# PEER block on one core: u of 32 more tokens from gathered rows, a dense u over 352 columns, 64 blocks ahead that alternate in the output, and a packed slot sum

## The chip, the cores and the metric

The kernel runs on one core of a Trainium2 chip. Its time is the device time of one execution in microseconds. Three executions of the kernel before took 1765.59, 1766.91 and 1767.95 us, median 1766.91. One further execution was profiled. Engines are called by their names in the profile: PE multiplies matrices, DVE (vector), ACT (scalar) and POOL (GpSimd) work on elements, SP issues most DMAs; POOL issues the gathers.

## The reference

One layer over 512 tokens of 1024 features in float32. First come two mixers (attention in bands of chunks, and an mLSTM); this part of the kernel, the front, is the same before and after. Then come the product-key experts:

```python
def peer_ffn(h, w_pq, sub_keys, u_exp, v_exp):          # 512 tokens, in blocks of 128
    q = (xb @ w_pq).reshape(128, 8, 2, 128)             # 8 heads, 2 halves of a key
    s = jnp.einsum("thpd,hpnd->thpn", q, sub_keys)      # 128 sub-keys for each half
    s_top, i_top = lax.top_k(s, 16)
    cand = s_top[:, :, 0, :, None] + s_top[:, :, 1, None, :]
    best, ci = lax.top_k(cand, 16)                      # 16 experts for each head
    e = i1 * 128 + i2                                   # of 128 x 128 = 16384
    gate = softmax(best)
    u, v = u_exp[e], v_exp[e]                           # 16384 rows of 1024 each
    act = gelu(einsum("thkd,td->thk", u, xb))
    return einsum("thk,thkd->td", gate * act, v)
```

Each token so uses 128 rows of u and 128 rows of v, out of 16384 rows in each table.

## The kernel before

Tokens 0 to 127 take their rows by gathering: for each of the 128 picks, one indirect DMA brings one row of 1024 floats for each token (512 KB), and DVE multiplies it with the token's features and sums (u; a "dot", tile `junk`), or adds it with the gate as factor (v, `sum_v`). This is `gathered`.

The other 384 tokens go densely through all 16384 experts, in 128 blocks of 128 experts. For one block e, `hidden` loads 128 rows of u (512 KB, tile `wst`), splits them into a high and a low half (`split`: ACT copies, then one subtraction on DVE or POOL, as the list `lanes["now"]` says), and forms 8 x 3 products of 128x384 on PE (`mm3`: high·high, low·high and high·low make up the precision of float32; tile `ps_act`), then gelu on ACT. `output` does the same with v's block (tile `vst`), after the hidden values have been multiplied by the gate weights (`gq`, result `ew`) and split in turn (`ehi`, `elo`): 18 products of 128x512 on PE into six accumulators (`acc`).

The gate weights of the dense tokens are a matrix of 16384 experts by 384 tokens, which `build` makes from one-hots: for each token one 128x128 matrix `oa` (the gate at the first index) and for four tokens one `o4` (the second index), multiplied on PE into `ps_g`, copied by ACT and written to DRAM as `gd`, to be read back as `gq`.

The order of the work is the order of the program: generators that are advanced in turn. `scores` (queries, top 16, `select` of the slots) and then `build` of token blocks 1, 2 and 3 run beside `ahead`, which already forms hidden values of 40 expert blocks (E1), 8 of them kept in SBUF and 32 written to DRAM (`ad`, read back as `aq`). In `output` then come 88 blocks that have both u and v to do (hot), and after them the 40 that have only v to do (cold). The gathers of tokens 0 to 127 are issued beside the output, 2.5 for each block (RATE_V).

The tiles have a fixed number of buffers (six for a gathered row, UR; four for a v block, VST; five halves of a split block, WB); an instruction that wants a buffer waits until its last reader is done.

## Time and profile before

| | before |
|---|---|
| runs | 1765.59, 1766.91, 1767.95 us (median 1766.91) |
| profiled execution | 1767.14 us, its span 1765.3 us |
| PE busy | 1705.3 us (97%), granted clock 0.988 |
| DVE busy | 1380.5 us (78%) |
| POOL, ACT busy | 832.6 us (47%), 806.3 us (46%) |
| moved by DMA | 413.35 MB, mean 234 GB/s |

The profiled execution's time is 1.84 us more than the span from the first to the last instruction, and 0.23 us more than the median of the three runs. An engine's busy time is the time in which at least one of its instructions ran; successive instructions of one engine overlap a little, so that a stream's pace is read from the distance of the starts rather than from the durations.

### The profile page before, as it was taken

The page shows a single profiled execution, that of the slowest core. Times are in us where ns is not written, and L with a number is a line of the kernel's source. Part 1 is how long each engine was busy: PE and PEld are TensorE (multiplying, and loading weights), DVE is VectorE, ACT ScalarE, POOL GpSimd, SP SyncE. Part 2 cuts the span into 40 slices and gives each one's busy share as a digit, 9 for nine tenths or more (in the row PEclk, how much of TensorE's full clock was granted, in tenths as well). Part 3 has the DMA queues.
Part 4 walks back from the last instruction along what each step waited for, and adds up shares of the span by engine and source line. Part 5 has one row for each costly group of instructions (what it writes and reads, how often), then busy time and mean ns, then how long its engine had stood idle before and what let it go on. Part 6 is the DMA issues. An engine that isn't in the chain of part 4 may idle for free.

```text
span 1765.3 us, 25467 instructions
## 1 busy us (share of the span) xinstructions
PE 1705.3 (97%) x8671; PEld 1486.5 (84%) x8671; DVE 1380.5 (78%) x2868; ACT 806.3 (46%) x1624; POOL 832.6 (47%) x692
## 2 busy tenths in 40 slices
PE   5999999999999897999999999999999999999997
PEld 4766678888798787999899999999999999998886
DVE  7557655675589998899477988899989898898445
ACT  4544545443543334998533443433434443434443
POOL 0000000000157676999455666677776677673221
PEclk9999999999999998999999999999999999999999
DMA  8423224563332333565998989989999989987653
GB/s 292 152 73 127 88 99 140 186 227 100 111 104 89 104 101 135 204 255 233 343 367 322 358 308 344 352 324 342 348 326 351 353 303 351 350 293 282 228 194 107
DMA packets 129940, 413.35 MB, mean 234 GB/s; under 512 B 12049, under 2 KB 38801, under 8 KB 128274
## 3 DMA queue, kind: packets, MB, share of 16 engines
q1 hardware_dynamic: 91218, 252.33, 41.3%
q0 software_dynamic: 38592, 159.40, 24.1%
q8 instruction: 68, 1.11, 0.2%
q14 instruction: 62, 0.51, 0.1%
HBM read 376.03 MB, written 35.66 MB: 233 GB/s over the span
## 4 chain that ended last, share of the span: by engine, by line
PE 80%; DVE 13%; DMA 4%; issue 1%; POOL 1%; ACT 1%; SPq 0%; DVEq 0%; ACTq 0%
PE acc L165 10%; PE acc L164 10%; PE acc L163 10%; PE ps_act L165 8%; PE ps_act L163 8%; PE ps_act L164 8%; PE ps_g L766 4%; DVE wlo L153 2%; DMA wst<-in_w_ada 1%; PE ps_ya L361 1%; PE ps_s L341 1%; PE ps_qk L163 1%; DVE i L648 1%; PE ps_qk L165 1%; DVE sc L649 1%
## 5 line engine op out<-in xcount | busy, mean ns | idle before, releaser
L150 ACT CAST whi<-wst 128x512 fp32r<-128x512 f32 x408 | 252.1, 621 | 482.6 <-PE ps_act L164 279.6
L165 PE MATMUL ps_act<-h2T_hi,wlo 128*128 128x384 f32 x1024 | 348.3, 340 | 5.0 <-DVE wlo L153 4.0
L163 PE MATMUL ps_act<-h2T_hi,whi 128*128 128x384 f32 x1024 | 347.0, 339 | 0.0
L164 PE MATMUL ps_act<-h2T_lo,whi 128*128 128x384 f32 x1024 | 346.8, 339 | 0.0
L164 PE MATMUL acc<-wlo,ehi 128*128 128x512 f32 x768 | 299.1, 391 | 0.0
L163 PE MATMUL acc<-whi,ehi 128*128 128x512 f32 x768 | 293.3, 390 | 3.3 <-ACT whi L150 3.3
L165 PE MATMUL acc<-whi,elo 128*128 128x512 f32 x768 | 286.9, 391 | 0.0
L153 DVE TENSOR_TENSOR wlo<-wst,whi 128x512 fp32r<-128x512 f32 x275 | 207.0, 756 | 98.2 <-ACT whi L150 91.1
L153 POOL TENSOR_TENSOR wlo<-wst,whi 128x512 fp32r<-128x512 f32 x133 | 184.4, 1393 | 180.9 <-ACT whi L150 174.9
L150 ACT CAST whi<-vst 128x512 fp32r<-128x512 f32 x256 | 158.0, 620 | 181.2 <-PE acc L165 137.9
L724 POOL DMA_INDIRECT vr<-in_v_r,ei x128 | 168.6, 1317 | 84.5 <-DVE sum_v L730 65.9
L710 POOL DMA_INDIRECT ur<-in_u_r,ei x128 | 153.5, 1199 | 115.3 <-DVE junk L713 93.6
L153 POOL TENSOR_TENSOR wlo<-vst,whi 128x512 fp32r<-128x512 f32 x85 | 131.0, 1541 | 151.7 <-ACT whi L150 136.1
L165 PEld LDWEIGHTS ps_act<-h2T_hi,wlo 128*128 128x128 f32 x1024 | 193.8, 189 | 7.3 <-DVE wlo L153 5.2
L163 PEld LDWEIGHTS ps_act<-h2T_hi,whi 128*128 128x128 f32 x1024 | 194.0, 189 | 3.7
L164 PEld LDWEIGHTS ps_act<-h2T_lo,whi 128*128 128x128 f32 x1024 | 193.9, 189 | 3.7
L730 DVE SCALAR_TENSOR_TENSOR sum_v<-vr,act,sum_v 128x1024 f32<-128x1024 f32 x127 | 181.2, 1427 | 1.2 <-DMA vr<-in_v_r,ei 0.4
L713 DVE SCALAR_TENSOR_TENSOR junk<-ur,h 128x1024 bf16<-128x1024 f32 x128 | 170.9, 1335 | 0.9
L163 PEld LDWEIGHTS acc<-whi,ehi 128*128 128x128 f32 x768 | 144.6, 188 | 31.5 <-ACT whi L150 3.6
L165 PEld LDWEIGHTS acc<-whi,elo 128*128 128x128 f32 x768 | 144.0, 188 | 30.4 <-DVE elo L841 0.2
L164 PEld LDWEIGHTS acc<-wlo,ehi 128*128 128x128 f32 x768 | 144.1, 188 | 28.5
L471 POOL TENSOR_SCALAR_AFFINE_SELECT mbd<-mbc 128x512 f32<-128x512 f32 x4 | 4.7, 1163 | 319.5 <-ACT mbc L469 319.5
(300 smaller groups left out, 3103.8 us busy)
## 6 DMA issues: line engine op xcount, KB each, us to landing
wst<-in_u_t SPq DMA_DIRECT2D x128, 512.0 KB
vst<-in_v_e SPq DMA_DIRECT2D x128, 512.0 KB
wst<-in_w_pieces SPq DMA_DIRECT2D x76, 512.0 KB
wst<-in_w_ada SPq DMA_DIRECT2D x48, 512.0 KB
gd<-gst POOLq DMA_DIRECT2D x12, 2048.0 KB
gq<-gd SPq DMA_DIRECT2D x16, 1536.0 KB
ad<-gelu SPq DMA_DIRECT2D x8, 768.0 KB
aq<-ad SPq DMA_DIRECT2D x8, 768.0 KB
```

The costliest lines, as they stand in the source:

```text
L150: nc.scalar.copy(hi, t[:, cs])
L153: e.tensor_tensor(out=lo, in0=t[:, cs], in1=hi.bitcast(F32), op=ALU.subtract)
L163: nc.tensor.matmul(o, a[0], b[0], start=first, stop=False)
L164: nc.tensor.matmul(o, a[0], b[1], start=False, stop=False)
L165: return nc.tensor.matmul(o, a[1], b[0], start=False, stop=last)
L341: nc.tensor.matmul(pss[:, :n], qaT[po : po + 64, cs], kaT[po : po + 64, hp, :n], start=True, stop=True)
L361: nc.tensor.matmul(psy[po : po + 64, cs], va[:, kt, h * 64 : (h + 1) * 64], pt[:, kt * P : (kt + 1) * P], start=kt == 0, stop=kt == qt,)
L710: nc.gpsimd.indirect_dma_start(out=t, out_offset=None, in_=u_r, in_offset=bass.IndirectOffsetOnAxis(ap=ei[:, j : j + 1], axis=0))
L713: nc.vector.scalar_tensor_tensor(junk(), t, 1.0, state["h2"][i], op0=ALU.mult, op1=ALU.mult, accum_out=act[:, j : j + 1])
L724: nc.gpsimd.indirect_dma_start(out=t, out_offset=None, in_=v_r, in_offset=bass.IndirectOffsetOnAxis(ap=ei[:, j : j + 1], axis=0))
L730: nc.vector.scalar_tensor_tensor(sum_v, t, act[:, j : j + 1], sum_v, op0=ALU.mult, op1=ALU.add)
L766: nc.tensor.matmul(ps[:, tt::4], oa, ob, start=True, stop=True)
```

## The change

1. Tokens 128 to 159 (TG = 32) now take u, not v, from gathered rows. The new `group` lays their 128 picks out as four groups of 32 tokens over the 128 partitions, so that 32 indirect DMAs of 128 rows do for 32 tokens. It needs small DMAs for the indices (`eg`, four for each head), for the results (`at`) and for three copies of the tokens' features; the result is multiplied into the gate weights of these tokens before they go into `build`.
2. The dense u so covers 352 columns (NU) in place of 384. The dense v keeps 384 (ND).
3. 64 blocks go ahead in place of 40, none kept in SBUF. In the output, groups of 8 hot and 8 cold blocks alternate.
4. The gathers of tokens 0 to 127 start in the build of token block 1 (RATE_0), go on beside the rest of the blocks ahead (RATE_A), and then take 2.6 for each hot and 1.25 for each cold block. The rows of `group` are gathered in the builds of token blocks 2 and 3 (RATE_G). `slowly` lets each gather be issued after the last subtraction (or slot operation) that DVE had been given by then.
5. `split` makes one subtraction of 1024 columns after the scores, and two of 512 in them. Its lanes are POOL, POOL, DVE in the scores and DVE alone from then on, in the output too (before: DVE, POOL, POOL until the output, DVE, DVE, POOL in it). The output takes experts in pairs: one multiplication by the gate weights of 704 columns, one split of 768.
6. One-hots: ACT takes a second one of each 16 tokens (`tt == 2`), and none for tokens 128 to 159.
7. `select`: one sum over products carries both parts of the slot (factor 64), and five operations of 64 elements take them apart; one 128x1024 product on POOL and one 128x1024 sum on DVE are gone, and three casts and copies pass from DVE to POOL.
8. Buffers: v blocks 4 to 3, gathered rows 6 to 5, split blocks five halves to three wholes, o4 6 to 4, one-hots 6 to 8 (POOL) and 16 to 12.

```diff
-VST, UR = 4, 6
+VST, UR = 3, 5
-E1 = 40
+TG = 32
+NU = S - P - TG
+ND = S - P
+E1 = 64
-RATE_S, RATE_B, RATE_V = 1.0, 0.15, 2.5
+RATE_S, TOP, RATE_G, RATE_B, RATE_0, RATE_A, HOT, COLD = 1.1, 2, 0.65, 0.4, 0.8, 1.0, 2.6, 1.25
-LANES_F = lambda nc: [nc.vector, nc.gpsimd, nc.gpsimd]
-LANES_V = lambda nc: [nc.vector, nc.vector, nc.gpsimd]
+LANES_S = lambda nc: [nc.gpsimd, nc.gpsimd, nc.vector]
+LANES_B = lambda nc: [nc.vector]
...
+    def group(cp):
+        slots = state["slots"][:TG, 1]
...
+        for h in range(8):
+            et = cp.tile([TG, TOPK], I32, tag="et", name="et")
+            nc.vector.scalar_tensor_tensor(et, slots[:, 0, h], float(P), slots[:, 1, h], op0=ALU.mult, op1=ALU.add)
+            hs = slice(h * NJ, (h + 1) * NJ)
+            for g in range(NR):
+                nc.sync.dma_start(eg[g * TG : (g + 1) * TG, hs], et[:, g * NJ : (g + 1) * NJ])
+            yield
+            for j in range(NJ):
+                dot_u(cp, eg, h * NJ + j, state["h2"][1], ag)
+                yield
...
+            ins = e.tensor_tensor(out=lo[:, cs], in0=t[:, cs], in1=hi[:, cs].bitcast(F32), op=ALU.subtract)
+            if e is nc.vector:
+                state["mark"] = ins.ins
...
+    def slowly(g):
+        while True:
+            with tc.issue_after(state["mark"]):
+                ended = next(g, 0) == 0
...
+            for i in (2, 3, 1):
+                if i == 1:
+                    drive((rows, 1))
+                    gate = state["slots"][:TG, 1, 2]
+                    nc.vector.tensor_mul(gate, gate, state["at"])
+                own = (slowly(gather), RATE_0) if i == 1 else (slowly(rows), RATE_G)
+                drive((paced(build(dp, i, state["slots"][:, i]), (side, RATE_B), own), 1))
+            drive((paced(side, (slowly(gather), RATE_A)), 1))
...
-        order = list(range(E1, P)) + list(range(E1))
+        hot, cold = ([list(range(e, e + GG, 2)) for e in r] for r in (range(E1, P, GG), range(0, E1, GG)))
+        while hot or cold:
+            for g in (hot, cold):
+                order += g.pop(0) if g else []
...
+                yield HOT if e >= E1 else COLD
...
-                    if tt == 0 and t4 % ACT_D < ACT_N:
+                    if (tt == 0 or (tt == 2 and t4 % 4 == 0)) and i * P + t >= P + TG:
                         nc.scalar.activation(oa, iota, AF.Abs, bias=neg[:, 0, t : t + 1])
...
-        nc.vector.tensor_copy(idx, i16)
+        nc.gpsimd.tensor_copy(idx, i16)
...
-        nc.vector.tensor_reduce(slots[:, :, 0, h], q, axis=AX.X, op=ALU.add)
-        nc.gpsimd.tensor_mul(m, m, bq(C_DOFF))
-        nc.vector.tensor_reduce(of, m, axis=AX.X, op=ALU.add)
-        nc.vector.tensor_sub(of, pf, of)
+        both = cp.tile([P, 4, TOPK], F32, tag="both", name="both")
+        nc.vector.tensor_reduce(both, q, axis=AX.X, op=ALU.add)
+        nc.vector.tensor_scalar(of, both, 1.0 / PACK, WHOLE, op0=ALU.mult, op1=ALU.add)
+        nc.vector.tensor_scalar_add(slots[:, :, 0, h], of, -WHOLE)
+        nc.vector.scalar_tensor_tensor(of, slots[:, :, 0, h], float(PACK), both, op0=ALU.mult, op1=ALU.subtract)
+        nc.vector.tensor_add(of, of, pf)
...
-        ps = bank(tag, "ps_act")[:, :ND]
-        proj_t(ps, u, [t[:, :, GT:] for t in h2T])
+        ps = bank(tag, "ps_act")[:, :NU]
+        proj_t(ps, u, [t[:, :, S - NU :] for t in h2T])
```

DVE's program inside the build before (one-hots `oa` and `o`, a half split `wlo` now and then):

```order
L750 TENSOR_TENSOR o_7731<-iota,sT 128x512
L153 TENSOR_TENSOR wlo<-wst,whi 128x512
L764 TENSOR_SCALAR oa<-iota,sT 128x128 x2
L750 TENSOR_TENSOR o_7748<-iota,sT 128x512
L764 TENSOR_SCALAR oa<-iota,sT 128x128 x2
L750 TENSOR_TENSOR o_7767<-iota,sT 128x512
```

DVE's program at a place of the build after (the one-hots at L799 and L784, a whole split at L150, and the dots of the 32 tokens' gathered rows, `junk,ag`):

```order
L784 TENSOR_TENSOR o_6480<-iota,sT 128x512
L799 TENSOR_SCALAR oa<-iota,sT 128x128
L712 SCALAR_TENSOR_TENSOR junk,ag<-ur,h_1_3828 128x1024
L799 TENSOR_SCALAR oa<-iota,sT 128x128
L784 TENSOR_TENSOR o_6501<-iota,sT 128x512
L799 TENSOR_SCALAR oa<-iota,sT 128x128
L150 TENSOR_TENSOR wlo<-wst,whi 128x1024
L712 SCALAR_TENSOR_TENSOR junk,ag<-ur,h_1_3828 128x1024
L784 TENSOR_TENSOR o_6518<-iota,sT 128x512
L799 TENSOR_SCALAR oa<-iota,sT 128x128 x2
L784 TENSOR_TENSOR o_6573<-iota,sT 128x512
```

Between the one-hots there now stand dots and whole splits.

POOL's program in the output before (the v rows' gathers `vr`, and POOL's share of the subtractions):

```order
L153 TENSOR_TENSOR wlo<-vst,whi 128x512
L724 DMA vr<-in_v_r,ei_8700 128x1024 x5
L153 TENSOR_TENSOR wlo<-vst,whi 128x512
L153 TENSOR_TENSOR wlo<-wst,whi 128x512
L724 DMA vr<-in_v_r,ei_8700 128x1024
L153 TENSOR_TENSOR wlo<-wst,whi 128x512
L724 DMA vr<-in_v_r,ei_8700 128x1024
L153 TENSOR_TENSOR wlo<-vst,whi 128x512
L724 DMA vr<-in_v_r,ei_8700 128x1024 x7
```

POOL's program after, from the last one-hot on (the gate weights' writes `gd`, the gathers of u and then of v for tokens 0 to 127):

```order
L799 TENSOR_SCALAR oa<-iota,sT 128x128
L807 DMA gd<-gst 128x4096
L704 DMA ur<-in_u_r,ei_8277 128x1024 x5
L807 DMA gd<-gst 128x4096
L704 DMA ur<-in_u_r,ei_8277 128x1024 x100
L704 DMA ur<-in_v_r,ei_8277 128x1024 x128
```

The subtractions are gone from POOL's queue, and gathers follow one another.

## Rows read from the trace of the kernel before

**Rows 1.** The busy time of each engine in seven stretches of the span: the front (mixers), the scores, the building of the gate weights, the rest of the blocks ahead, the hot blocks of the output, its cold blocks, the tail. Columns: stretch, its length in us, then busy us and number of instructions of PE, PE's weight loads, DVE, ACT and POOL, PE's granted clock as a share, the DMA engines' busy share, GB/s.

```profile
0.00:467.90 467.90, 441.00 (x1993) 339.29 (x1993) 293.33 (x701) 214.98 (x453) 9.99 (x17) 0.98 0.44 148
467.90:704.90 237.00, 217.46 (x1127) 195.33 (x1127) 216.56 (x921) 95.20 (x180) 150.02 (x152) 0.96 0.31 102
704.90:846.10 141.20, 140.83 (x1083) 140.34 (x1082) 132.64 (x285) 128.86 (x319) 134.97 (x123) 1.00 0.61 236
846.10:875.00 28.90, 25.63 (x150) 25.31 (x149) 6.98 (x14) 10.95 (x22) 11.53 (x11) 1.00 0.93 340
875.00:1583.50 708.50, 708.50 (x3570) 644.37 (x3571) 622.46 (x777) 281.81 (x511) 481.53 (x362) 1.00 0.93 337
1583.50:1755.40 171.90, 171.86 (x758) 141.84 (x757) 102.06 (x161) 72.43 (x137) 44.60 (x29) 1.00 0.60 211
1755.40:1765.30 9.90, 0.00 (x0) 0.00 (x0) 6.42 (x15) 2.11 (x8) 0.00 (x0) 0.70 0.42 159
```

**Rows 2.** The chain of work that ended last, its shares of the span by engine (part 4 of the page).

```profile
PE 80%; DVE 13%; DMA 4%; issue 1%; POOL 1%; ACT 1%; SPq 0%; DVEq 0%; ACTq 0%
```

**Rows 3.** Waits in the whole span: who waited on which line, for whom; us in total, times, longest us.

```profile
POOL ur L710 <- DVE junk L713: 93.6, 68, 4.8
...
PE ps_slT L739 <- DVE slots L688: 7.5, 1, 7.5
```

**Rows 4.** Three rows of PE's timeline in the hot blocks (start us, duration us). Between the first and the second of them stand 13 more rows of ps_act, between the second and the third six more of acc, none with idle time before it.

```profile
999.78 0.33 PE L164 MATMUL ps_act<-h2T_lo,whi 128*128 128x384 f32 x1
...
1002.20 0.39 PE L163 MATMUL acc<-whi,ehi 128*128 128x512 f32 x1
...
1003.82 0.40 PE L164 MATMUL acc<-wlo,ehi 128*128 128x512 f32 x1
```

**Rows 5.** PE's groups in the stretch 875.0 to 1583.5 (hot blocks); two more groups of 674 and two of 516, one for each of the other two products, stand beside them. Columns: tiles and shapes, count, busy us, mean ns of one, idle us before them.

```profile
L163 PE MATMUL ps_act<-h2T_hi,whi 128*128 128x384 f32 x674 | 226.4, 336 | 0.0
...
L163 PE MATMUL acc<-whi,ehi 128*128 128x512 f32 x516 | 200.7, 391 | 3.3 <-ACT whi L150 3.3
```

**Rows 6.** The same in the stretch 1583.5 to 1755.4 (cold blocks); two more groups of 252 stand beside it.

```profile
L163 PE MATMUL acc<-whi,ehi 128*128 128x512 f32 x252 | 92.7, 389 | 0.0
```

**Rows 7.** DVE's groups in the stretch 467.9 to 704.9 (scores), shapes kept apart.

```profile
L153 DVE TENSOR_TENSOR wlo<-wst,whi 128x512 fp32r<-128x512 f32 x26 | 32.6, 1254 | 9.0 <-ACT whi L150 9.0
...
L690 DVE TENSOR_REDUCE of<-m 128x64 f32<-128x1024 f32 x8 | 9.6, 1200 | 0.0
L656 DVE CAST idx<-i 128x128 f32<-128x128 uint32 x8 | 7.0, 879 | 0.2
...
L670 DVE COPY dl<-idx 128x4 f32<-128x4 f32 x8 | 4.3, 535 | 0.1
...
L691 DVE TENSOR_TENSOR of<-pf,of 128x64 f32<-128x64 f32 x8 | 3.4, 428 | 0.0
...
L668 DVE CAST pf<-pos 128x64 f32<-128x64 uint32 x8 | 2.5, 314 | 0.2
```

**Rows 8.** One of POOL's groups in the same stretch.

```profile
L689 POOL TENSOR_TENSOR m<-m,cst 128x1024 f32<-128x1024 f32 x8 | 20.4, 2551 | 0.2
```

**Rows 9.** DVE's one-hots in the stretch 704.9 to 846.1 (build).

```profile
L764 DVE TENSOR_SCALAR oa<-iota,sT 128x128 f32<-128x128 f32 x185 | 74.3, 445 | 0.5 <-PE ps_g L766 0.5
L750 DVE TENSOR_TENSOR o<-iota,sT 128x512 f32<-128x512 f32 x90 | 64.6, 727 | 7.9 <-ACT sT L741 7.9
```

**Rows 10.** DVE's timeline inside the build (start us, duration us; x2 is two instructions drawn together).

```profile
721.14 0.59 DVE L764 TENSOR_SCALAR oa<-iota,sT 128x128 f32<-128x128 f32 x2
721.66 0.68 DVE L750 TENSOR_TENSOR o<-iota,sT 128x512 f32<-128x512 f32 x1
722.26 0.59 DVE L764 TENSOR_SCALAR oa<-iota,sT 128x128 f32<-128x128 f32 x2
```

**Rows 11.** One piece of the chain of waits in the build, in order of time (start us, length us).

```profile
758.27 1.78 PE ps_g L766 x16
```

**Rows 12.** DVE's timeline in the hot blocks.

```profile
998.87 2.35 DVE L153 TENSOR_TENSOR wlo<-vst,whi 128x512 fp32r<-128x512 f32 x1 [0.36 <-ACT whi L150]
1001.14 1.21 DVE L713 SCALAR_TENSOR_TENSOR junk<-ur,h 128x1024 bf16<-128x1024 f32 x1
...
1002.28 0.68 DVE L153 TENSOR_TENSOR wlo<-wst,whi 128x512 fp32r<-128x512 f32 x1
1002.89 1.21 DVE L713 SCALAR_TENSOR_TENSOR junk<-ur,h 128x1024 bf16<-128x1024 f32 x1
```

**Rows 13.** POOL's timeline in the same place.

```profile
999.35 1.30 POOL L153 TENSOR_TENSOR wlo<-vst,whi 128x512 fp32r<-128x512 f32 x1
```

**Rows 14.** DVE's two groups that read gathered rows, in the stretch 875.0 to 1583.5.

```profile
L730 DVE SCALAR_TENSOR_TENSOR sum_v<-vr,act,sum_v 128x1024 f32<-128x1024 f32 x121 | 171.5, 1417 | 1.2 <-DMA vr<-in_v_r,ei 0.4
L713 DVE SCALAR_TENSOR_TENSOR junk<-ur,h 128x1024 bf16<-128x1024 f32 x128 | 170.9, 1335 | 0.9
```

**Rows 15.** PE's timeline at the end of the scores, around its longest wait there.

```profile
686.10 0.48 PE L739 MATMUL ps_slT<-ident,slots 128*128 128x128 f32 x1 [7.51 <-DVE slots L688]
...
687.01 0.52 PE L163 MATMUL ps_act<-h2T_hi,whi 128*128 128x384 f32 x1
687.34 0.52 PE L164 MATMUL ps_act<-h2T_lo,whi 128*128 128x384 f32 x1
```

**Rows 16.** What the DMA engines moved, in 40 equal slices of the span, 44.1 us each (part 2 of the page).

```profile
GB/s 292 152 73 127 88 99 140 186 227 100 111 104 89 104 101 135 204 255 233 343 367 322 358 308 344 352 324 342 348 326 351 353 303 351 350 293 282 228 194 107
```

More of the change, by code (lines that the diff above doesn't have):

```diff
@@ L595, in branches @@
         h2T = features("h2T")
[L596 removed]
+        h2 = [hpool.tile([P, D], F32, tag=f"row{i}", name=f"h2_{i}") for i in range(2)]
         state["h2T"], state["h2"] = h2T, h2
@@ new lines, in output @@
+            whb, wlb = (x.rearrange("p i (b t) -> p b i t", t=TB) for x in (whi, wlo))
+            nc.scalar.copy(whb, w)
+            nc.vector.tensor_sub(wlb, w, whb.bitcast(F32))
+            for i in range(2):
+                v = split(load(v_e[e + i], "vst", VST, vp), vp, VB)
+                last = e == order[-1] and i == 1
+                late.append((e == order[0] and i == 0, last, whi[:, i, :], wlo[:, i, :], v))
+                if len(late) > 1 and not last:
+                    x = late.pop(0)
+                    for n in range(2):
+                        for j in range(nt):
+                            rows_of_v(j, n, *x)
+                yield HOT if e >= E1 else COLD
@@ L935, in tile_block @@
             nc.sync.dma_start(gtd, gt2[:1, :])
-            main, side = front(dp, dp, h2T), ahead(up, h2T, held)
-            lanes["now"] = LANES_F(nc)
-            n, due = 0, 0.0
-            for _ in main:
-                n += 1
-                due += RATE_S if n <= 16 else RATE_B
-                while due >= 1.0:
-                    due -= 1.0
-                    next(side, None)
-            drive((side, 1))
-            lanes["now"] = LANES_V(nc)
+            side, rows, gather = ahead(up, h2T), group(cp), gathered(cp, 0)
+            lanes["now"] = LANES_S(nc)
+            drive((paced(scores(dp, h2T), (side, RATE_S)), 1))
+            for _ in range(TOP):
+                next(side, None)
+            lanes["now"], state["cuts"] = LANES_B(nc), 1
+            for i in (2, 3, 1):
[6 more added lines that the diff above has]
+            drive((paced(side, (slowly(gather), RATE_A)), 1))
         if stop == "u":
             return
-        with pool("vpool") as vp, pool("rpool") as rp:
-            gather = gather_side(rp)
-            with tc.issue_after(state["marks"][MARK]):
-                next(gather)
-                next(gather)
-            paced(output(rp, vp, h2T, held), gather, RATE_V)
+        with pool("vpool") as vp:
+            drive((paced(output(cp, vp, h2T), (slowly(gather), None)), 1))
             drive((gather, 1))
```

209 lines of the change are left out of this document (102 added, 107 removed).

## The prediction

> **What bounds the kernel now.** I read the table of stretches first [rows 1]. From 875.0 to 1755.4 us PE is busy all the time (708.50 of 708.5 and 171.86 of 171.9 us), so the output is PE's own work. The build is nearly the same (140.83 of 141.2). In the scores PE idles 19.5 of 237.0 us; there DVE has 216.56 us of work and most of the chain. Over the whole span the chain is 80% PE and 13% DVE [rows 2]. The question is therefore what PE is given less of, and whether the engines that now serve it keep up.
>
> Next the pace of PE, from the distance of starts. Fourteen products of 384 columns take 1002.20 − 999.78 = 2.42 us, 173 ns each; seven of 512 take 1.62 us, 231 ns [rows 4]. Whole stretches are the better measure. The cold blocks give 171.9/(3 × 252) = 0.2274 us for 512 columns [rows 1, 6]. The hot blocks then give (708.5 − 1548 × 0.2274)/2022 = 0.1763 us for 384, waits included [rows 1, 5]. The slope is 0.0511/128 = 0.40 ns per column; the 32 columns are worth 12.8 ns, and one product of 352 should take 0.1635 us.
>
> **What leaves PE.** 128 blocks × 24 products × 12.8 ns = 39.3 us. v stays at 384 tokens, and the one-hot products stay. This is the only work that PE loses; all else moves work between stretches or between engines. The bounds are nothing saved and 0.45 ns per column, from the two timeline paces (231 − 173 over 128): 44 us.
>
> By the Trainium skill ("TensorE: Matmul & The Clock Gate", section Back-to-back issue gap) a sustained stream of weight loads and products is spaced by both, at about 81 ns for 128 columns and 131 ns for 512. Its slope, 0.13 ns per column, would make the saving only an estimated 13 us. The trace's 227 ns for 512 disagrees, so I take the rows.
>
> **Scores, 237.0 to about 239 us.** DVE sets the pace. Removed are the second sum L690 (9.6 us), the casts and copies (7.0, 4.3, 2.5) and L691 (3.4): 26.8 us [rows 7]. Added are 40 operations of 64 elements. L691, of this size, took 0.43 us with POOL busy beside it [rows 7]; `oa`, with twice the elements, stands 0.26 us from the next [rows 10]. I take 0.26, 10 us; the other end is 17. Program order puts 22 half and 10 whole subtractions there, in place of 26 halves: 22 × 1.254 + 10 × 1.2 − 32.6 = +7 us. Eight dots at 1.25 us add 10, four index operations about 1.5. The sum is 237.0 − 26.8 + 10 + 7 + 10 + 1.5 = 238.7. POOL loses L689 (20.4 us, [rows 8]) and gains the casts, which DVE then waits for: bounds 230 to 250. PE stands behind DVE here anyway: its 217.46 us [rows 1] were 384 × 0.2274 + 595 × 0.1763 and 25 of small products; now they are 384 × 0.2274 + 694 × 0.1635 + 25 = 226.
>
> **Build, 141.2 to about 213 us.** By program order 680 products of u lie between the first and the last one-hot product, where 309 lay before. PE needs 768 one-hot products at 0.111 us (16 in 1.78, [rows 11]) and 680 × 0.1635: 85 + 111 = 196 us. DVE needs more. One-hots: 96 `o4` and 178 `oa`. Starts show two `oa` in 0.52 and one `o4` in 0.60 us [rows 10], which gives 96 × 0.60 + 178 × 0.26 = 104 us. Means of the stretch, 727 and 445 ns [rows 9], overlap somewhat; scaled to DVE's busy time they give about 134. POOL's computing, which went on in 130 of 141 us, will cover about half of the new stretch, so I take the middle, 120. To this come 28 whole subtractions and 45 dots. A dot alone is 1.14 us from start to start (1001.14 to 1002.28, [rows 12]) and 1.335 on average [rows 14]; a whole subtraction reads the same two operands of 1024. At 1.2 us both: 34 + 54 = 88 us. With 5 us of small operations and waits the build is 213 us, DVE-bound, with PE idle for some 17 us. The bounds are 196 (PE) and 134 + 73 × 1.36 = 233.
>
> What is queued behind a dot: if the gathered row is late, the one-hots and subtractions behind it wait, and PE for them. Gathers stand some five or six of the 96 one-hot steps ahead in program order, 11 to 13 us at 213/96 = 2.2 us for each; five buffers cover five dots. I cost this at nothing. Without that lead each dot would wait for its issue and transfer. The 32 index DMAs, the four of the results and the three copies of features are small and lie on SP, behind loads that run ahead of PE; nothing waits for them as long as that holds. ACT forms 110 one-hots where it formed 90 and 28 casts of 1024 for 27 of 512: its 128.86 us [rows 1] grow to some 170 of 213.
>
> **Rest ahead, 28.9 to 50 us:** 306 products × 0.1635. Twelve dots and 14 subtractions, 31 us on DVE, hide behind it. The stretch's 25.63 us of PE and its 3.3 us of waiting at the change of pools [rows 1, 5] were the 28.9.
>
> **Output, 880.4 to 751.5 us.** 2304 × 0.2274 + 1392 × 0.1635 = 523.9 + 227.6. DVE then does every subtraction. A half took 2.35 us beside POOL's subtraction and 0.61 without it [rows 12, 13]; POOL computes nothing there now. DVE has 181 whole subtractions and 95 dots at 1.15, 127 v rows at 1.2 to 1.43 [rows 14], and 126 pair operations at about 0.8 us: 206 + 109 + 165 + 101 = 581 of 751 us, where it was 622 of 708. POOL's 93.6 us of waits for a dot [rows 3] only show that buffers, not POOL, hold the gathers; that costs nothing.
>
> DMA is the doubt. At 0.524 MB for a block or a gather, eight cold blocks read 4.19 MB of v, 1.44 of `aq` (8 × 128 × 352 floats), 1.57 of `gq` (384) and ten gathers, 5.24: 12.4 MB in 8 × 18 × 0.2274 = 32.7 us, 380 GB/s. The best slice so far is 367 GB/s [rows 16], the hot stretch 337 at a share of 0.93 [rows 1]. Hot groups (u, v, `gq`, 20.8 gathers) ask 20.9 MB in 64 us, 325 GB/s. At 367 a cold group needs 33.9 us, 1.1 more, 9 us in eight groups; what the buffers hold from the hot group before takes some of it off, down to nothing. I take 4.5.
>
> The Trainium skill ("DMA: Bandwidth & Descriptors", section Where 436 GB/s comes from) has HBM bind at about 358 GB/s for one core. The slice of 367 lies above this, so no ceiling of 358 shows here. By it a cold group would take an estimated 34.7 us, 15 in all, and the sum would be 10 us higher.
>
> **Sum.** 467.9 + 239 + 213 + 50 + 751.5 + 4.5 + 9.9 (tail) = 1735.8 us of span, against 1765.3; with the 1.84 us around the span **1738 us**. The profiled execution before lies 0.23 us above the median of the runs, so no correction is due.
>
> **Rivals.**
> *Gathers come late (slower).* In the scores and the build, 53 dots stand in DVE's only queue ahead of work that PE wants. The gain of 29 us is gone when each waits 29/53 = 0.55 us. For it: `slowly` holds each gather behind a DVE subtraction, and in the first builds the small index DMAs stand in SP's queue behind loads of 512 KB. Against it: dots waited only 0.9 us in 128 [rows 14]. At 0.8 us each: 1738 + 42 = 1780 us.
> *The columns pay nothing or little,* because something other than the columns spaces the products. For it: each product loads weights. Against it: one-hot products, with a weight load each, follow at 111 ns [rows 11]. Nothing saved: 1738 + 39 = 1777. With 4 ns in place of 12.8 for 32 columns: 1738 + 26 = 1764.
> *Cold groups are DMA-bound.* At the sustained 337 GB/s each needs 36.8 us, 4 us more, 32 in all, and 1738 − 4.5 + 32 = 1766; at 350 it is 1753. DVE stalls on a dot and PE on a subtraction.
> *The build is PE-bound,* one-hots running at 104 us and dots at 1.14: 1738 − 17 = 1721.
> *Many small idle times lower PE's clock.* After 7.51 us without work PE's products followed at 0.33 instead of 0.17 us [rows 15]. In the DVE-bound build waits are of a microsecond or less, so I give this no case of its own; it belongs to the first.
>
> **Numbers.** My forecast (1728 to 1746): 0.50. PE-bound build, about 1721: 0.13. DMA-bound cold groups, 1746 to 1766: 0.19, mostly in its lower half. Gathers late, 1770 and more: 0.08. Columns that don't pay, 1764 to 1777: 0.05. Others, either side: 0.05. The range 1714 to 1763 leaves out some 0.2. About 0.2% is what a measurement of this kernel can tell from no change (1763.4 to 1770.4): faster 0.82, same 0.07, slower 0.11.
>
> **What would show it.** The products of 352 columns spaced 160 to 164 ns; the build's stretch some 213 us with DVE busy nearly throughout and PE waiting for `ps_g`'s one-hots; subtractions of 1024 at 1.14 us in the output; PE full there, with waits of a few us at the start of cold groups if DMA is short. I am wrong if dots wait on gathered rows in the build, if PE idles more than some 10 us in the output, or if the spacing stays at 173 ns.

## The result, and the profile of the changed kernel

| | before | changed |
|---|---|---|
| median | 1766.91 us (1764.48 to 1769.43, 5 runs) | 1757.45 us (1755.98 to 1759.75, 5 runs) |
| ratio | | 0.9948, 95% interval 0.9933 to 0.9962 |
| span of the profiled execution | 1765.3 us | 1754.6 us |
| moved by DMA | 413.35 MB | 440.99 MB |

The change makes the kernel faster, by 9.5 us where I had forecast 29. The time lies in my range; the size of the gain is a third of the forecast.

The table of stretches of the changed kernel, with the same columns as [rows 1]: front, scores, build, rest ahead, output, tail (the output has one row now, since hot and cold blocks alternate).

```profile
0.00:473.20 473.20, 441.29 (x1993) 339.82 (x1993) 293.33 (x701) 210.67 (x454) 9.88 (x18) 0.98 0.45 148
473.20:714.00 240.80, 225.33 (x1234) 203.47 (x1233) 210.96 (x935) 96.73 (x187) 145.95 (x169) 0.98 0.41 136
714.00:941.50 227.50, 205.40 (x1457) 202.49 (x1455) 193.35 (x399) 163.72 (x368) 215.81 (x153) 0.96 0.80 293
941.50:994.00 52.50, 49.77 (x310) 48.97 (x308) 30.67 (x38) 19.20 (x27) 18.56 (x13) 1.00 1.02 407
994.00:1741.40 747.40, 747.35 (x3696) 654.12 (x3696) 599.50 (x650) 264.19 (x321) 322.44 (x219) 1.00 0.91 332
1741.40:1754.60 13.20, 0.00 (x0) 0.00 (x0) 6.64 (x14) 2.25 (x8) 0.00 (x0) 0.70 0.44 159
```

Against the terms of my sum:

| stretch | before | forecast | measured | missed by |
|---|---|---|---|---|
| front | 467.9 | 467.9 | 473.2 | +5.3 |
| scores | 237.0 | 239 | 240.8 | +1.8 |
| build | 141.2 | 213 | 227.5 | +14.5 |
| rest ahead | 28.9 | 50 | 52.5 | +2.5 |
| output | 880.4 | 751.5 + 4.5 | 747.4 | −8.6 |
| tail | 9.9 | 9.9 | 13.2 | +3.3 |
| span | 1765.3 | 1735.8 | 1754.6 | +18.8 |

The output came out better than forecast, and the build is where most of the rest went. There PE worked 205.40 of 227.5 us and DVE 193.35, so neither is the bound that I had named. The busiest is POOL: 215.81 us. It was busy in every third of the build alike, while PE's granted clock was below full in the first two; in the last third PE is as full as POOL:

```profile
714.00:790.00 76.00, 61.89 (x429) 60.39 (x428) 58.12 (x122) 50.57 (x115) 72.24 (x49) 0.94 0.70 250
790.00:865.00 75.00, 69.81 (x494) 69.17 (x493) 64.05 (x132) 56.99 (x132) 71.50 (x51) 0.95 0.81 301
865.00:941.50 76.50, 73.70 (x536) 72.93 (x536) 71.18 (x147) 56.16 (x122) 72.07 (x55) 1.00 0.89 329
```

POOL's groups in that stretch (a row is line, engine, operation, tiles, count, then busy us, mean ns of one, idle us before them):

```profile
L799 POOL TENSOR_SCALAR oa<-iota,sT 128x128 f32<-128x128 f32 x96 | 152.3, 1592 | 1.4
L704 POOL DMA_INDIRECT ur<-in_u_r,ei x26 | 36.2, 1392 | 5.3 <-issue 3.7 <-DVE oa L799 1.2 <-DVE junk L712 0.3
L704 POOL DMA_INDIRECT ur<-in_u_r,eg x20 | 23.8, 1192 | 5.1 <-issue 3.9 <-DVE oa L799 0.8 <-DVE o L784 0.3
```

The 96 one-hots that POOL forms took 1592 ns each, and POOL hardly waited for anything else: its idle time is 11.7 us, most of it "issue". DVE's 193.35 us of work and its 34.1 us of waits, nearly all at dots, make up the whole 227.5. Here stand two of those who waited for POOL's one-hots and gathers, DVE and PE, from the waits of the build (who, for whom; us, times, longest):

```profile
DVE junk L712 <- DMA ur<-in_u_r,eg: 24.3, 4, 7.5
...
PE ps_g L801 <- DVE o L784: 11.4, 4, 4.9
...
PE ps_g L801 <- POOL oa L799: 8.4, 5, 2.8
...
DVE junk L712 <- DMA ur<-in_u_r,ei: 5.3, 1, 5.3
```

Dots waited 24.3 us at four gathered rows of tokens 128 to 159 (`eg`), and 5.3 us at one of tokens 0 to 127 (`ei`). The chain of waits shows one of them whole: POOL's one-hots end, the gather is issued, its transfer takes 4.5 us, and PE's one-hot products follow.

```profile
819.74 2.93 POOL oa L799 x3
822.83 4.50 DMA ur<-in_u_r,eg
...
829.41 2.04 PE ps_g L801 x8
```

### The profile page after: what moved, and what is told of

Same layout as the page of the kernel before. It is cut to its first block, busy times and chain, and to the rows that moved or that the text cites. A ratio compares the mean times of both kernels' runs of the same rounds, so it can differ in the third digit from the quotient of the medians.

```text
span 1754.6 us, 24732 instructions
## 1 busy us (share of the span) xinstructions
PE 1669.1 (95%) x8679; PEld 1448.9 (83%) x8679; DVE 1334.5 (76%) x2732; ACT 756.8 (43%) x1361; POOL 712.6 (41%) x570
## 2 busy tenths in 40 slices
DMA packets 139613, 440.99 MB, mean 251 GB/s; under 512 B 15489, under 2 KB 42241, under 8 KB 137954
## 3 DMA queue, kind: packets, MB, share of 16 engines
q8 instruction: 68, 1.11, 0.3%
## 4 chain that ended last, share of the span: by engine, by line
PE 50%; DVE 11%; DMA 6%; POOL 3%; issue 3%; ACT 1%; DVEq 0%; SPq 0%; POOLq 0%; ACTq 0%
PE acc L160 10%; PE acc L162 10%; PE acc L161 10%; PE ps_act L162 5%; PE ps_act L160 5%; PE ps_act L161 5%; PE ps_g L801 3%; POOL oa L799 2%; DVE wlo L150 2%; DMA ur<-in_u_r,eg 1%; DMA ur<-in_u_r,ei 1%; DMA wst<-in_u_t 1%; DVE junk L712 1%; DMA vst<-in_v_e 1%; DVE i L648 1%
## 5 line engine op out<-in xcount | busy, mean ns | idle before, releaser
L147 ACT CAST whi<-wst 128x512 fp32r<-128x512 f32 (+1 forms) x300 | 222.6, 773 | 408.0 <-PE ps_act L161 187.7
L162 PE MATMUL ps_act<-h2T_hi,wlo 128*128 128x352 f32 x1024 | 336.8, 329 | 12.5 <-DVE wlo L150 7.3
L160 PE MATMUL ps_act<-h2T_hi,whi 128*128 128x352 f32 x1024 | 333.6, 326 | 0.7 <-ACT ew L815 0.7
L161 PE MATMUL ps_act<-h2T_lo,whi 128*128 128x352 f32 x1024 | 333.8, 326 | 0.0
L150 DVE TENSOR_TENSOR wlo<-wst,whi 128x512 fp32r<-128x512 f32 (+1 forms) x252 | 235.8, 949 | 96.1 <-ACT whi L147 92.7
L704 POOL DMA_INDIRECT ur<-in_v_r,ei x128 | 191.4, 1496 | 205.0 <-DVE sum_v L764 185.3
L147 ACT CAST whi<-vst 128x1024 fp32r<-128x1024 f32 x128 | 132.4, 1048 | 129.7 <-PE acc L162 61.4
L150 DVE TENSOR_TENSOR wlo<-vst,whi 128x1024 fp32r<-128x1024 f32 x128 | 154.7, 1219 | 36.6 <-ACT whi L147 35.9
L764 DVE SCALAR_TENSOR_TENSOR sum_v<-ur,act,sum_v 128x1024 f32<-128x1024 f32 x127 | 162.5, 1280 | 7.5 <-DMA ur<-in_v_r,ei 6.6
L160 PEld LDWEIGHTS acc<-whi,ehi 128*128 128x128 f32 x768 | 143.0, 188 | 28.9 <-ACT ehi L866 2.3
L799 POOL TENSOR_SCALAR oa<-iota,sT 128x128 f32<-128x128 f32 x96 | 152.3, 1592 | 1.4
```

The costliest lines, as they stand in the source:

```text
L147: nc.scalar.copy(hi[:, cs], t[:, cs])
L150: ins = e.tensor_tensor(out=lo[:, cs], in0=t[:, cs], in1=hi[:, cs].bitcast(F32), op=ALU.subtract)
L160: nc.tensor.matmul(o, a[0], b[0], start=first, stop=False)
L161: nc.tensor.matmul(o, a[0], b[1], start=False, stop=False)
L162: return nc.tensor.matmul(o, a[1], b[0], start=False, stop=last)
L704: nc.gpsimd.indirect_dma_start(out=t, out_offset=None, in_=src, in_offset=bass.IndirectOffsetOnAxis(ap=ei[:, j : j + 1], axis=0))
```

## The experiments

All of them are edits of the changed kernel unless said otherwise; "changed" is its 1757.45 us and its profile. Times are medians; each ratio is to the kernel before as it ran beside that version.

**Half of POOL's one-hots (pool_half).**

```diff
-                    own = tt == 1
+                    own = tt == 1 and t4 % 2 == 0
...
-                    if (tt == 0 or (tt == 2 and t4 % 4 == 0)) and i * P + t >= P + TG:
+                    if (tt == 0 or (tt == 1 and not own) or (tt == 2 and t4 % 4 == 0)) and i * P + t >= P + TG:
```

> POOL forms every second of its one-hots only (48 of 96); ACT takes the others, DVE for tokens 128 to 159. The result stays that of the reference. Theory P: the build of the changed kernel (227.5 us) is set by POOL's queue, where slow one-hots (96 at 1.59 us, 152 us) and the issue of 46 gathers (60 us) fill 216 us, so that gathers are issued late and the dots wait. Then POOL falls to some 140 us, the dots' 30 us of waits nearly vanish, the build comes down to what DVE (193) and PE (196) need, 200 to 208 us, and the whole to about 1735 (0.983 of the kernel before, against 0.995 for the change). Theory D: gathered rows come late because the DMA engines are busy (share 0.80 to 0.89 there). Then the dots wait as before and the build stays at 222 to 230, the whole at 1753 to 1760. Theory V: DVE's own work sets the build. Then the same, or 4 us slower, since DVE gets four more one-hots.

1742.42 us, ratio 0.9869 (0.9847 to 0.9891): 15 us faster than the changed kernel. Its stretches from the scores to the rest ahead:

```profile
473.00:721.10 248.10, 228.20 (x1237) 206.54 (x1237) 217.41 (x946) 98.70 (x192) 153.21 (x171) 0.96 0.43 141
721.10:950.20 229.10, 219.54 (x1582) 217.41 (x1581) 206.12 (x416) 196.34 (x462) 150.93 (x111) 0.99 0.88 328
950.20:981.00 30.80, 29.46 (x178) 29.17 (x177) 12.90 (x14) 11.75 (x17) 4.02 (x5) 1.00 1.01 372
```

Theory P named a right cause and the wrong place for the gain. The build's stretch did not get shorter (229.1 us), but PE was busy 219.54 us in it, 14 more, with more blocks of u done there; so the rest ahead fell from 52.5 to 30.8 us. The scores took 7.3 us more, at a granted clock of 0.96 in place of 0.98; why stayed open. The three stretches together took 508.0 us against 520.8. POOL is down to 150.93 us and now waits 53.8 us for DVE; DVE (206.12), ACT (196.34) and PE (219.54) share the bound. The dots' waits fell from 29.6 to 15.9 us, and did not nearly vanish. Theory D is out: the DMA share rose from 0.80 to 0.88. So is theory V, since DVE has four one-hots more and the kernel is faster.

**Dots that wait for no row (loose_dots).**

```diff
-                dot_u(cp, eg, h * NJ + j, state["h2"][1], ag)
+                row(cp, u_r, eg, h * NJ + j)
+                c = h * NJ + j
+                nc.vector.scalar_tensor_tensor(
+                    junk(), state["h2"][0], 1.0, state["h2"][1], op0=ALU.mult, op1=ALU.mult, accum_out=ag[:, c : c + 1]
+                )
```

> The 32 gathers of tokens 128 to 159 are issued as in the changed kernel, but their dots read a tile that is always there, so that no dot waits for a gathered row (the picks' products of these 32 tokens are so left out of the result). Theory P: POOL's queue is as full as before and sets the pace through its one-hots, so the build falls little: from 227.5 to 218 or more, the whole to 1748 or more. Theory D (late rows alone): the 24 us that dots waited for these rows go, build about 203 us, the whole about 1733. Theory V: no change, since DVE does the same work.

1757.87 us, ratio 0.9956 (0.9940 to 0.9973): no change, although the 24.3 us of waits for rows of tokens 128 to 159, which the list of waits of the changed kernel names first, are gone. The same three stretches took 527.0 us. The test isn't clean: the dots of tokens 0 to 127 now waited longer, so that the waits at dots went from 29.6 to 15.5 us only. In the build PE's one-hot products waited for POOL in place of DVE (groups, then waits):

```profile
L803 POOL TENSOR_SCALAR oa<-iota,sT 128x128 f32<-128x128 f32 x95 | 133.6, 1413 | 3.9 <-ACT sT L779 2.8
```

```profile
DVE junk L712 <- DMA ur<-in_u_r,ei: 15.5, 5, 6.2
PE ps_g L805 <- POOL oa L803: 14.7, 10, 2.8
```

**The same dots, and the gathers not issued either (no_gathers).** (An edit of loose_dots.)

```diff
-                row(cp, u_r, eg, h * NJ + j)
```

> As the version whose dots of tokens 128 to 159 read a tile that is always there, but their 32 gathers are not issued either (their picks' products are left out of the result). DVE's work is that of the changed kernel. If POOL's queue sets the build's pace as the sum of one-hots and gather issues, 24 issues of 1.2 us, 29 us, leave it in the build, and the whole comes to 1757 - 20 to - 29, 1728 to 1738. If the slow one-hots alone set the pace, whatever stands between them, it stays at 1750 to 1758.

1751.92 us, ratio 0.9921 (0.9897 to 0.9945): about 5 us faster, much less than the 20 to 29 of a sum of one-hots and issues. So the issues are the smaller part: this is the second case. POOL was busy 185.95 of the 211.1 us of this build and did wait now (21.0 us before its one-hots), so that it no longer sets the pace alone. The one-hots' mean stays as in the changed kernel without any gather of these tokens beside them:

```profile
L802 POOL TENSOR_SCALAR oa<-iota,sT 128x128 f32<-128x128 f32 x96 | 150.3, 1572 | 21.0 <-ACT sT L778 14.2 <-PE ps_g L804 5.6
```

**The gathers without their dots (no_dots).** (An edit of loose_dots; the unused results are set to zero.)

```diff
-                c = h * NJ + j
-                nc.vector.scalar_tensor_tensor(
-                    junk(), state["h2"][0], 1.0, state["h2"][1], op0=ALU.mult, op1=ALU.mult, accum_out=ag[:, c : c + 1]
-                )
```

> The changed kernel with the 32 gathers of tokens 128 to 159 issued on POOL as before, but without their 32 dots on DVE (their picks' products are left out of the result). Some 24 dots of 1.14 us so leave the build, 27 us of DVE instructions that read two operands. If these are what slows POOL's one-hots (96 at a mean of 1.59 us in the changed kernel, 1.57 without the gathers, 0.78 at their fastest), the mean falls to about 1.33 us, POOL's work in the build by some 25 us, and the whole comes to 1730 to 1742. If POOL's one-hots are slow for a reason of their own, the mean stays at 1.5 to 1.6 and the whole is 1745 or more.

1738.84 us, ratio 0.9839 (0.9816 to 0.9862). The mean of POOL's one-hots fell to what was expected:

```profile
L800 POOL TENSOR_SCALAR oa<-iota,sT 128x128 f32<-128x128 f32 x96 | 126.3, 1324 | 1.2
```

All 96, as the least, the median and the longest of them (ns), in the kernel before, the changed kernel, this one and loose_dots:

```profile
L764 POOL TENSOR_SCALAR oa<-iota,sT x96: 781/1126/2283, 699.2 to 841.1; 128x128 f32<-128x128 f32 x96
```

```profile
L799 POOL TENSOR_SCALAR oa<-iota,sT x96: 782/1362/4519, 712.9 to 934.6; 128x128 f32<-128x128 f32 x96
```

```profile
L800 POOL TENSOR_SCALAR oa<-iota,sT x96: 780/1128/3235, 707.1 to 909.6; 128x128 f32<-128x128 f32 x96
```

```profile
L803 POOL TENSOR_SCALAR oa<-iota,sT x96: 780/1162/7601, 723.5 to 940.6; 128x128 f32<-128x128 f32 x96
```

The least is 0.78 us everywhere. The medians don't tell the theories apart: loose_dots, which has all its dots, is nearly at the median of before, too. The means do so better, but versions with all dots lie between 1.44 us (old_select, below) and 1.61 (hot_first). DVE's own load falls as well here (160.80 us in a build of 212.8), so the 18.6 us in the whole are not POOL's alone.

The trace itself separates the theories, one-hot by one-hot. In the changed kernel 16 of the 96 overlap no DVE instruction that reads two operands; they took 0.78 to 0.84 us. The other 80 took 1.75 us on average. The overlap with such instructions is 1.11 us of the mean of 1.59, and what remains is 0.48 us; in the kernel before it is 0.66 of 1.14, in loose_dots 1.00 of 1.48 and here 0.80 of 1.32, and 0.47 to 0.53 us remain. Seven one-hots of the kernel before ran wholly beside DVE's one-hots with one tensor operand and took no more than 0.80 to 0.87 us. So it is not DVE's work as such, but its two-operand instructions, dots, subtractions and `o4` alike.

How it looks can be read in one place of the changed kernel, POOL's and DVE's timelines side by side (start us, duration us):

```profile
748.07 4.52 POOL L799 TENSOR_SCALAR oa<-iota,sT 128x128 f32<-128x128 f32 x1
```

```profile
747.99 1.21 DVE L150 TENSOR_TENSOR wlo<-wst,whi 128x1024 fp32r<-128x1024 f32 x1
749.13 1.21 DVE L712 SCALAR_TENSOR_TENSOR junk<-ur,h 128x1024 bf16<-128x1024 f32 x1
...
750.27 1.21 DVE L150 TENSOR_TENSOR wlo<-wst,whi 128x1024 fp32r<-128x1024 f32 x1
751.41 0.68 DVE L784 TENSOR_TENSOR o<-iota,sT 128x512 f32<-128x512 f32 x1
```

One one-hot of POOL lasts 4.52 us, and 4.08 of them lie beside four DVE instructions that read two operands from SBUF (three of 1024 columns, one one-hot of 512). In the kernel before DVE had only the `o4` of 0.60 us and a few half subtractions there; in the changed one it has dots and whole subtractions besides. A straight line through the 96 one-hots gives 0.63 us and 0.87 us more for each microsecond of such overlap: POOL loses nearly the whole of it. The Trainium skill says in "GPSIMD Engine Reference", section Specifications, that POOL's interfaces to SBUF are shared with DVE, with contention from DVE instructions that have two SBUF inputs. The 1.75 us beside such instructions and at most 0.84 without them agree.

**384 columns again (cols384).**

```diff
-        ps = bank(tag, "ps_act")[:, :NU]
-        proj_t(ps, u, [t[:, :, S - NU :] for t in h2T])
-        nc.scalar.activation(g, ps, AF.Gelu_apprx_tanh)
+        ps = bank(tag, "ps_act")[:, :ND]
+        proj_t(ps, u, [t[:, :, S - ND :] for t in h2T])
+        nc.scalar.activation(g, ps[:, ND - NU :], AF.Gelu_apprx_tanh)
```

> The dense u products keep 384 columns, all else is the changed kernel (the 32 extra columns are not used). If the 32 columns are worth 12.8 ns for each product wherever PE is the bound: 2392 products outside the build give 30.6 us, and the 680 in the build are hidden as long as POOL sets its pace there: 1757 + 31 = 1788. If the build shows them too: 1797. If columns pay nothing: 1757. At 4 ns for 32 columns: 1767 to 1770.

1808.99 us, ratio 1.0250 (1.0230 to 1.0270): the columns are worth 51.5 us, more than any of the cases. Its output:

```profile
1016.60:1789.60 773.00, 772.98 (x3722) 679.98 (x3720) 605.34 (x653) 270.07 (x326) 316.92 (x219) 1.00 0.88 320
```

```profile
L162 PE MATMUL ps_act<-h2T_hi,wlo 128*128 128x384 f32 x473 | 159.0, 336 | 0.0
```

With 3 × 473 products, less one, and 2304 of 512 columns at 0.2274: (773.0 − 523.9)/1418 = 0.1757 us for 384 columns. The changed kernel's output gives (747.4 − 523.9)/1392 = 0.1606 for 352:

```profile
L160 PE MATMUL ps_act<-h2T_hi,whi 128*128 128x352 f32 x464 | 149.3, 322 | 0.0
```

The difference is 15.1 ns, 46 us over 3072 products. From the scores to the rest ahead this version took 547.4 us in place of 520.8: 26.6 more, although 26 of its products lie in the output instead. At 15.1 ns each the other 1654 would take 25.0 us more, and without the 26 the stretches should have grown by 20.8. So nothing of the columns was hidden there, and the time lies above both of my cases, 1788 and 1797. The build itself grew by 4.8 us (to 232.3), the scores by 14.8. A build that POOL alone paces would have hidden its 10 us; POOL was busy only 206.65 us of this one and waited 9.8 us in it for one head's indices. How much of the changed kernel's build PE would still take without POOL is therefore open. A slope of 4 ns for 32 columns, an estimate from the 81 ns for 128 columns and 131 ns for 512 that the Trainium skill gives ("TensorE: Matmul & The Clock Gate", section Back-to-back issue gap), does not hold here.

**The slot sum as before (old_select).** (The casts and copies are on DVE again, too.)

```diff
-        both = cp.tile([P, 4, TOPK], F32, tag="both", name="both")
-        nc.vector.tensor_reduce(both, q, axis=AX.X, op=ALU.add)
...
+        nc.vector.tensor_reduce(slots[:, :, 0, h], q, axis=AX.X, op=ALU.add)
+        nc.gpsimd.tensor_mul(m, m, bq(C_DOFF))
+        nc.vector.tensor_reduce(of, m, axis=AX.X, op=ALU.add)
+        nc.vector.tensor_sub(of, pf, of)
```

> The packed slot sum alone is undone: two sums and two products with the comparison, casts on DVE again. If DVE sets the pace of the scores (it is busy 211 of 240.8 us there), its 26.8 us come back and 10 go: 17 us slower, about 1774. If PE (225 of 240.8 us) or POOL (146) carries the stretch, it is 0 to 6 us slower, 1757 to 1763.

1767.63 us, ratio 1.0004 (0.9986 to 1.0023): 10 us slower than the changed kernel, between the two cases. Scores to rest ahead took 534.4 us, 13.6 more. This fits DVE setting the pace of the scores, with five small operations that cost more than I had put down: 15.0 us in the changed kernel in place of 10, against 27.9 here for the sum, the casts, the copy and the subtraction that they replace. The size is loose: the ten runs lie between 1757.74 and 1774.09 us, at a granted clock of 0.976 to 0.982, where the changed kernel had 0.983 to 0.985.

**Hot blocks first, then cold (hot_first).**

```diff
-        while hot or cold:
-            for g in (hot, cold):
-                order += g.pop(0) if g else []
+        for g in hot + cold:
+            order += g
```

> The changed kernel with its output in the order of before: all 64 hot blocks, then all 64 cold ones, in place of groups of 8 in turn. Hot blocks ask for 325 GB/s and 6.2 of 8.0 us of DVE for each, cold ones with the same rate of gathers 380 GB/s. If the turns let buffers carry over the cold blocks' demand, PE waits in the long cold stretch and the whole is 10 to 25 us slower, 1767 to 1782. If DMA was never the limit: 1754 to 1760.

1769.64 us, ratio 1.0014 (0.9997 to 1.0032): the turns are worth 12 us. The two halves of this output:

```profile
997.10:1471.00 473.90, 473.87 (x2490) 428.93 (x2491) 387.63 (x442) 169.11 (x209) 221.66 (x160) 1.00 0.94 339
1471.00:1754.10 283.10, 276.72 (x1208) 225.42 (x1207) 214.74 (x209) 98.20 (x112) 90.96 (x60) 1.00 0.85 309
```

```profile
ACT whi L147 <- DMA vst<-in_v_e: 46.4, 21, 6.9
```

```profile
1502.00:1679.00 177.00, 170.70 (x743) 138.25 (x742) 145.50 (x135) 57.95 (x61) 73.87 (x49) 1.00 0.98 364
```

PE has no wait in the hot half and some 6 us of them in the cold one; ACT waited there 21 times for a block of v. PE's waits lie in the 177 us of the third row, where gathers still run; there the DMA engines moved 364 GB/s at a share of 0.98. So DMA is short in the cold blocks when nothing is carried over, and the turns hide it.

**POOL's share of the output's subtractions back (lanes_out).** (Halves of 512 columns in the output, every third on POOL, as in the kernel before.)

```diff
+        lanes["now"], state["cuts"] = [nc.vector, nc.vector, nc.gpsimd], 2
         with pool("vpool") as vp:
```

> The changed kernel with the output's subtractions as before: halves of 512, every third one on POOL. POOL's subtraction slows DVE's beside it (2.35 for 0.61 us in the kernel before) and stands in the queue of the gathers. If PE stays covered by what DVE has to spare (599 of 747 us), as my forecast has it, the output stays at 745 to 750 us, 1755 to 1760. If DVE's slower work shows, the output is 10 us or more longer.

1769.47 us, ratio 1.0021 (1.0001 to 1.0041): 12 us slower, the second case; the profiled execution, 1773.82 us, is 4 us slower still. DVE's work in the output grows although POOL takes a third of the subtractions away from it:

```profile
998.40:1758.80 760.40, 748.17 (x3676) 650.97 (x3675) 673.21 (x707) 275.81 (x499) 478.95 (x341) 1.00 0.90 325
```

```profile
L764 DVE SCALAR_TENSOR_TENSOR sum_v<-ur,act,sum_v 128x1024 f32<-128x1024 f32 x127 | 197.2, 1553 | 2.9 <-DMA ur<-in_v_r,ei 1.6
L150 DVE TENSOR_TENSOR wlo<-vst,whi 128x512 fp32r<-128x512 f32 x174 | 147.4, 871 | 22.5 <-ACT whi L147 21.5 <-issue 0.9
L712 DVE SCALAR_TENSOR_TENSOR junk<-ur,h 128x1024 bf16<-128x1024 f32 x95 | 141.0, 1484 | 1.7 <-DMA ur<-in_u_r,ei 0.8
```

DVE is busy 673.21 us in place of 599.50, since a v row takes 1553 ns here and a dot 1484, where the changed kernel shows 1280 and 1218 in its output. PE waits 8.0 us by way of ACT's `ehi`, which waits for DVE's multiplication by the gate weights, where it waited 2.0 in the changed kernel. How much of the 12 us comes from POOL's share and how much from the halves was not separated. PE's row here, and DVE's two rows in the changed kernel:

```profile
L160 PE MATMUL acc<-whi,ehi 128*128 128x512 f32 x768 | 274.5, 392 | 9.6 <-ACT ehi L866 8.0 <-ACT whi L147 1.6
```

```profile
L764 DVE SCALAR_TENSOR_TENSOR sum_v<-ur,act,sum_v 128x1024 f32<-128x1024 f32 x127 | 162.5, 1280 | 7.5 <-DMA ur<-in_v_r,ei 6.6
...
L712 DVE SCALAR_TENSOR_TENSOR junk<-ur,h 128x1024 bf16<-128x1024 f32 x96 | 116.9, 1218 | 1.1 <-DMA ur<-in_u_r,ei 0.4
```

**Half of POOL's one-hots, and another buffer for the tail (half_xr).** (An edit of pool_half.)

```diff
-        xr = cp.tile([P, D], F32, tag="ur", name="xr", bufs=UR)
+        xr = wpool.tile([P, D], F32, tag="wst", name="xr", bufs=WST)
```

> The version with half of POOL's one-hots, and besides it the rows of x that the last step adds (xr) come into a buffer of the weights' ring in place of the ring of gathered rows, which the change cut from six buffers to five. If the tail (13.1 to 13.3 us from the last product in the changed kernel and all its variants, 9.9 before) is longer because DVE waits there for the output's DMA to leave a buffer of that ring, the tail goes back to about 10 us and the whole to 1739. If it has another cause, the tail stays at 13 and the whole at 1742.

1740.04 us, ratio 0.9833 (0.9809 to 0.9857). The tail is back at its length of before, so the cause of its 3.3 us is settled. In the changed kernel's chain DVE waits there for the output's DMA:

```profile
1742.20 3.53 DMA out<-o
```

```profile
1735.00:1745.10 10.10, 0.01 (x1) 0.00 (x0) 6.42 (x13) 2.27 (x8) 0.00 (x0) 0.67 0.42 156
```

This version beats both kernels: by 1.7% the kernel before (the ratio) and by some 1% the changed one (1740.04 against 1757.45 us). Against pool_half its 2.4 us are within the noise of four runs each.

**All indices ahead of the first dot (half_early).** (An edit of half_xr.)

```diff
             for g in range(NR):
                 nc.sync.dma_start(eg[g * TG : (g + 1) * TG, hs], et[:, g * NJ : (g + 1) * NJ])
-            yield
+        yield
+        for h in range(8):
             for j in range(NJ):
```

> The version with half of POOL's one-hots and the moved xr, and besides it the indices of all eight heads are formed and sent before the first dot of tokens 128 to 159, in place of each head's just ahead of its four gathers. The result stays that of the reference. In the version without this the dots still wait some 16 us in the build, nearly all at the first gather of a head. If that is the way of each head's indices (an operation on DVE, four small DMAs on SP, then the gather), the waits go and the whole is 5 to 12 us faster, 1728 to 1735. If the waits come from POOL's slow one-hots or from the gathers' own transfers, nothing changes: 1738 to 1742. If gathers issued earlier stand in POOL's queue ahead of the last product of the slots, the scores get longer: 1745 or more.

1739.95 us, ratio 0.9839 (0.9811 to 0.9867): nothing gained. The dots' waits in the build fell from 16.8 us in half_xr to 8.1, and scores to rest ahead from 512.6 to 499.7 us, but the output took 753.9 us in place of 747.5: about a block that had been done ahead is now in it, and PE waits 7.5 us at its start by way of a first block of v that comes late. Half of the 12.9 us won ahead of the output is lost so. The rest says little, since the profiled execution of half_xr, 1746.83 us, lies 6.8 us above its median, and this one's at its median.

**The kernel before once more (before_again).**

> The kernel before, once more, for the length of the front, which the change does not touch: 467.9 us in the profile shown, 469 to 475 in the profiles of the changed kernel and its variants. If this is chance, it lies between 468 and 474 here; if the change makes it longer by something that runs beside it, it is 466 to 469.

Its span is 1764.3 us, its front 466.7 us, 467.9 in the first profile [rows 1]. In the changed kernel and its ten variants the front is 469.2 to 474.9 us, 472.9 on average. So it is hardly chance that the front is longer by some 5 us. PE falls behind in several small steps, and the instructions of the front ran in a slightly different order in the two kernels. Which edit does this stayed open; it wasn't tried.

## Why the prediction was right or wrong

The sign was right and the gain three times too large. Of the 18.8 us missed in the span, 14.5 lie in the build and 8.6 in the front and the tail, which I had carried over; the scores and the rest ahead add 4.3, and the output gave 8.6 back. Point by point:

- **The bound of the build: wrong, and the step that failed.** "DVE needs more", I wrote, and bounded the build by PE and DVE alone. POOL's one-hots went into the sum only as something that slows DVE, computing in "about half of the new stretch"; they took 152.3 us of it, two thirds. I never made POOL's own sum: 96 one-hots and 46 gather issues. POOL had been busy 134.97 of 141.2 us in the build before [rows 1], and that row alone should have made me do it. At some 1.14 us for a one-hot, its mean before, and 1.3 for an issue it would still have come to only 169 us, below the bound; the size needs the second half of the mechanism, which I had seen from one side only. I read how POOL slows DVE ([rows 12, 13]) and did not ask how DVE slows POOL. The runs showed 1.59 us for a one-hot, 1.32 without the dots of 32 tokens, and 0.78 to 0.84 for those that overlap no two-operand instruction of DVE. POOL was busy 215.81 of 227.5 us, and taking half of its one-hots away gained 15 us. It isn't the only bound: PE's work is close behind, as cols384 and no_gathers show.
- **DVE's own sum: too high.** I had 208 us of instructions and 5 of small operations and waits; DVE was busy 193.35 us and waited 34.1. The 15 us too many hid half of the waits that I had left out, which was luck.
- **"I cost this at nothing": wrong.** Dots that wait in the build were also my first sign of being wrong. A gather's lead of five or six one-hot steps was counted in program order. Each of those steps has a POOL one-hot in it, so that the lead shrank as POOL fell behind; this is read from one place of the chain. Yet the late rows look like a sign and not the price: with half of these waits gone in loose_dots nothing was gained, and with half of them gone by way of POOL's one-hots 15 us.
- **The rival "gathers come late"** came true in its mechanism and not in its price: dots waited 29.6 us in the build for rows of both kinds, 24.3 and 5.3, at five dots of 46. By the 29 us that I had set for no gain nothing should have been left, and 9.5 us were.
- **The columns: right mechanism, mis-sized term.** 12.8 ns for 32 columns against 15.1 measured, and 51.5 us in the whole against 39.3. I drew a line through 384 and 512 columns; per column the three paces are 0.456 ns (352), 0.458 (384) and 0.444 (512), so that between 352 and 384 simple proportion was the better guide: 0.1763 × 352/384 = 0.1616. The rival that columns don't pay fell.
- **The output: right, a little too high.** 747.4 us with PE full; DVE's 599.50 us stand against the forecast 581. DMA cost nothing there, since the alternation carries the cold blocks over: the 4.5 us were not needed, and hot_first shows what they would have become. The rival of DMA-bound cold groups is so right about a kernel without the alternation, though its 1753 us at 350 GB/s was a slip: 12.44 MB take 35.5 us there, 2.8 more for each group, which makes 1756.
- **"POOL computes nothing there now": right in its direction, wrong in its price.** I costed the change of lanes in the output at nothing, since PE had been full before with POOL's share. lanes_out shows 12 us. DVE there has 673.21 us to do beside 748 of PE's, and in the hot groups, with 2.6 gathers for each block, more than on average; that this is where the cover ended is argued and not shown.
- **Scores: right in sum** (240.8 against 239), by terms that partly cancel. Small operations took 15 us instead of 10, PE was busy 225.33 us as forecast (226).
- **Clock:** I gave it no case because waits would be "of a microsecond or less". PE's longest waits in the build were of 4.9 us, and its granted clock was 0.94 and 0.95 in the first two thirds. What the clock alone cost was not measured.
- **Tail and front** I had carried over unchanged. The tail's 3.3 us come from the buffer that the change took from the ring of gathered rows, an edit that I listed and did not follow to its last user. The front's 5 us stay open.

## What to carry to other kernels

Make the sum of busy time for every engine in a stretch to which work is moved, also for those that "only" help, and price an instruction by what will run beside it there, in both directions. A wait that leads the list can be a symptom: try to take the cause of the lateness away, and not only the wait. And where buffers are cut, follow them to the last place in the program that uses them.
